# The last quarter of an HBM-to-HBM copy in 8 KB stretches in place of 32 KB

## The chip, the cores and the metric

The kernel runs on one core of a Trainium2 chip. The metric is device time in microseconds, the median of several runs. A profile of one execution, taken by the hardware profiler, stands beside it. It records every instruction and every packet that the core's 16 DMA engines move.

## The reference, and what it computes

A mixture-of-experts layer gives each token a position in its expert's buffer, and drops tokens whose position is not under the capacity. The reference is two lines:

```python
mask = token_positions < capacity          # (16, 1024) int, capacity 256
return (x * mask[..., np.newaxis]).astype(np.float32)   # x: (16, 1024, 512) float32
```

The positions are drawn from 0 to 255, so on these inputs every token is kept, and the output equals x: 33.55 MB to be read and as many to be written.

## The kernel before, in words

The kernel bets on that. It copies x to the output straight from HBM to HBM (HBM is the chip's main memory), without passing through a compute engine. Meanwhile it counts the kept tokens, and only if one is dropped does it go over the data again.

*The copy (L77 to L83).* The 16,384 tokens are laid out as 128 rows of 128 tokens, each token 512 floats, so a row is 256 KB of consecutive bytes. One transfer takes C = 16 tokens of every row: 128 stretches of 32 KB, 256 KB apart, 4 MB together. Eight of them cover the tensor. They go in turn to the two hardware queues that engines own: even ones are issued by SyncE (sp; queue q1 in the profile), odd ones by ScalarE (act; queue q10). All of them raise one semaphore, s_copy, by 16 each when they have landed.

*The order.* The copies and the load of the positions (L72, on ScalarE, ahead of its first copy) are collected in the list "early" and moved to the front of the program (L86 to L95), ahead of the barriers that start the other engines. So each of the two engines issues its transfers one after another and then meets the others at these barriers (L189 and L41 in the profile). Nothing else decides the order. A transfer waits for no other, and the queues may work on them as fast as they can.

*The decision (L97 to L139).* VectorE compares the positions with the capacity (ge, lt, low, keep at L103 to L115), sums keep along each row (kept, L119), TensorE adds up the 128 rows (total, L123), and VectorE makes a flag of it (drop_i, L125). SyncE, ScalarE and VectorE each load the flag (L133) and branch on it. The branch (L140 to L161) would load 4 MB at a time through SBUF (the on-chip memory), multiply by keep and store it, after waiting for the whole copy. Here it is never taken, and no instruction of it stands in the profile.

*The end (L164 to L172).* GpSimd clears the semaphores, waits until s_copy has its full count, 16 times the number of copies, and takes that count off again (L172). That wait is the end of the program.

Of the kernel before, what the change touches and what calls it, by code (L numbers as in the profile page):

```python
# [1 line left out]

# [4 lines left out]


@with_exitstack
def kernel(  # L10
    ctx: ExitStack,
    tc: tile.TileContext,
    x: bass.AP,
    token_positions: bass.AP,
    capacity: bass.AP,
    out: bass.AP,
):
    nc = tc.nc
    P = nc.NUM_PARTITIONS
    fp32 = mybir.dt.float32  # L20
    i32 = mybir.dt.int32
    Alu = mybir.AluOpType

    x_f = x.flatten_outer_dims()
    out_f = out.flatten_outer_dims()
    N, D = x_f.shape
    n_per_p = N // P
    cap = float(int(capacity))
    x_r = x_f.rearrange("(p n) d -> p n d", p=P)
    out_r = out_f.rearrange("(p n) d -> p n d", p=P)  # L30
    tp_i32 = token_positions.rearrange("b s -> (b s)").bitcast(i32)

    sp = nc.sync
    act = nc.scalar
    ve = nc.vector
    pe = nc.tensor
    gp = nc.gpsimd


    tc.close()  # L40
    tc.compile()  # L41

    def sbuf(name, shape, dtype):
        return ctx.enter_context(nc.sbuf_tensor(name, shape, dtype)).ap()

    tp = sbuf("tp", [P, 2 * n_per_p], i32)
    ge = sbuf("ge", [P, n_per_p], fp32)
    lt = sbuf("lt", [P, n_per_p], fp32)
    low = sbuf("low", [P, n_per_p], fp32)
    keep = sbuf("keep", [P, n_per_p], fp32)  # L50
    kept = sbuf("kept", [P, 1], fp32)
    ones = sbuf("ones", [P, 1], fp32)
    drop_i = sbuf("drop_i", [1, 1], i32)
    total = ctx.enter_context(nc.psum_tensor("total", [1, 1], fp32)).ap()
    F = 16
    NBUF = 2
    n_fix = n_per_p // F
    xts = [sbuf(f"xt{b}", [P, F, D], fp32) for b in range(NBUF)]

    s_copy = nc.alloc_semaphore("s_copy")  # L60
    s_tp = nc.alloc_semaphore("s_tp")
    s_ve = nc.alloc_semaphore("s_ve")
    s_pe = nc.alloc_semaphore("s_pe")
    s_ld = [nc.alloc_semaphore(f"s_ld{b}") for b in range(NBUF)]
    s_mul = nc.alloc_semaphore("s_mul")
    s_st = [nc.alloc_semaphore(f"s_st{b}") for b in range(NBUF)]
    s_done = nc.alloc_semaphore("s_done")

    n_copy = 0
    early = []  # L70

    load_tp = act.dma_start(out=tp, in_=tp_i32.rearrange("(p w) -> p w", p=P))  # L72
    early.append(load_tp.then_inc(s_tp, 16).ins)

    C = 16  # L77
    for k in range(n_per_p // C):
        ins = (sp, act)[k % 2].dma_start(
            out=out_r[:, k * C : (k + 1) * C, :], in_=x_r[:, k * C : (k + 1) * C, :]  # L80
        ).then_inc(s_copy, 16)
        early.append(ins.ins)
        n_copy += 1  # L83


    home = nc.cur_bb.bb  # L86
    first_bb = nc.cur_f.blocks[0]
    first_sp = next(
        k for k, i in enumerate(first_bb.instructions) if i.engine == mybir.EngineType.SP
    )  # L90
    names = [i.name for i in early]
    home.instructions = [i for i in home.instructions if i.name not in names]
    first_bb.instructions = (
        first_bb.instructions[:first_sp] + early + first_bb.instructions[first_sp:]
    )  # L95

    lo = tp[:, 0 : 2 * n_per_p : 2]  # L97
    hi = tp[:, 1 : 2 * n_per_p : 2]


    ve.memset(ones, 1.0).then_inc(s_ve, 1)  # L101
    ve.wait_ge(s_tp, 16)
    ve.tensor_scalar(  # L103
        out=ge, in0=lo, scalar1=0.0, scalar2=None, op0=Alu.is_ge
    ).then_inc(s_ve, 1)
    ve.wait_ge(s_ve, 2)
    ve.scalar_tensor_tensor(  # L107
        out=lt, in0=lo, scalar=cap, in1=ge, op0=Alu.is_lt, op1=Alu.mult
    ).then_inc(s_ve, 1)
    ve.wait_ge(s_ve, 3)  # L110
    ve.scalar_tensor_tensor(  # L111
        out=low, in0=hi, scalar=0.0, in1=lt, op0=Alu.is_equal, op1=Alu.mult
    ).then_inc(s_ve, 1)
    ve.wait_ge(s_ve, 4)
    ve.scalar_tensor_tensor(  # L115
        out=keep, in0=hi, scalar=0.0, in1=low, op0=Alu.is_lt, op1=Alu.add
    ).then_inc(s_ve, 1)
    ve.wait_ge(s_ve, 5)
    ve.tensor_reduce(  # L119
        out=kept, in_=keep, axis=mybir.AxisListType.X, op=Alu.add  # L120
    ).then_inc(s_ve, 1)
    pe.wait_ge(s_ve, 6)
    pe.matmul(out=total, lhsT=ones, rhs=kept, start=True, stop=True).then_inc(s_pe, 1)  # L123
    ve.wait_ge(s_pe, 1)
    ve.tensor_scalar(  # L125
        out=drop_i, in0=total, scalar1=float(N) - 0.5, scalar2=None, op0=Alu.is_lt
    ).then_inc(s_ve, 1)


    for e in (sp, act, ve):  # L130
        e.wait_ge(s_ve, 7)
    ET = mybir.EngineType
    drop = nc.values_load(  # L133
        drop_i[0:1, 0:1],
        engines=[ET.SP, ET.Activation, ET.DVE],
        min_val=0,
        max_val=1,
        skip_runtime_bounds_check_because="a comparison gives 0 or 1",
    )  # L139
    with nc.If(drop):  # L140
        for u in range(n_fix):
            b = u % NBUF
            if u >= NBUF:
                sp.wait_ge(s_st[b], 16 * (u // NBUF))
            sp.dma_start(out=xts[b], in_=x_r[:, u * F : (u + 1) * F, :]).then_inc(s_ld[b], 16)
            ve.wait_ge(s_ld[b], 16 * (u // NBUF + 1))
            for j in range(F):
                c = u * F + j
                ve.tensor_scalar(
                    out=xts[b][:, j, :],  # L150
                    in0=xts[b][:, j, :],
                    scalar1=keep[:, c : c + 1],
                    scalar2=None,
                    op0=Alu.mult,
                ).then_inc(s_mul, 1)
            if u == 0:
                act.wait_ge(s_copy, 16 * n_copy)
            act.wait_ge(s_mul, (u + 1) * F)
            act.dma_start(out=out_r[:, u * F : (u + 1) * F, :], in_=xts[b]).then_inc(s_st[b], 16)
        for b in range(NBUF):  # L160
            act.wait_ge(s_st[b], 16 * (n_fix // NBUF))  # L161


    for e in (sp, act, ve):  # L164
        e.sem_inc(s_done, 1)
    gp.wait_ge(s_done, 3)
    own = [s_tp, s_ve, s_pe, *s_ld, s_mul, *s_st, s_done]
    ids = sorted(s.num for s in own)
    assert ids == list(range(ids[0], ids[-1] + 1))
    gp.sem_clear(range(ids[0], ids[-1] + 1))  # L170
    gp.wait_ge(s_copy, 16 * n_copy)
    gp.sem_inc(s_copy, -16 * n_copy)  # L172


# [1 line left out]
_INS = ['x', 'token_positions', 'capacity']  # L176
_OUTS = [((16, 1024, 512), 'float32')]

_NUMBERS = {'capacity': 256}


# [26 lines left out]
```

## Time and profile before

| What | Value |
|---|---|
| Time, median of 3 runs | 104.15 us (103.99 to 104.38) |
| Span of the profiled execution | 104.3 us |
| Busy: VectorE, TensorE, GpSimd | 1.5, 0.2, 0.2 us |
| DMA packets, bytes, mean rate | 1297, 33.69 MB, 323 GB/s |
| Queue q1 (SyncE's), q10 (ScalarE's) | 48.6%, 49.4% of 16 engines' span |
| From issue to landing of a copy, shortest, median, longest | 25.0, 65.2, 101.7 us |

A DMA rate in this profile counts each byte once, though a copy from HBM to HBM reads and writes it. The share of a queue is the time that its packets took, over the span of all 16 DMA engines. The packet records have a start and a duration each. A 4-byte packet is a semaphore's increment, sent by each engine at the end of its part of a transfer. Time from issue to landing is long, because all transfers are issued in the first microseconds and stand in line.

### The profile page before, as it was taken

The page shows a single profiled execution, that of the slowest core. Times are in us where ns is not written, and L with a number is a line of the kernel's source. Part 1 is how long each engine was busy: PE and PEld are TensorE (multiplying, and loading weights), DVE is VectorE, ACT ScalarE, POOL GpSimd, SP SyncE. Part 2 cuts the span into 40 slices and gives each one's busy share as a digit, 9 for nine tenths or more (in the row PEclk, how much of TensorE's full clock was granted, in tenths as well). Part 3 has the DMA queues.
Part 4 walks back from the last instruction along what each step waited for, and adds up shares of the span by engine and source line. Part 5 has one row for each costly group of instructions (what it writes and reads, how often), then busy time and mean ns, then how long its engine had stood idle before and what let it go on. Part 6 is the DMA issues. An engine that isn't in the chain of part 4 may idle for free. (4 is left out here: it accounts for less than half of the span.)

```text
span 104.3 us, 70 instructions
## 1 busy us (share of the span) xinstructions
PE 0.2 (0%) x2; PEld 0.1 (0%) x2; DVE 1.5 (1%) x7; POOL 0.2 (0%) x4
## 2 busy tenths in 40 slices
PE   0000000000000000000000000000000000000000
PEld 0000000000000000000000000000000000000000
DVE  0230000000000000000000000000000000000000
POOL 0000000000000000000000000000000000000000
DMA  8999989989989989999899997998997999989984
GB/s 251 402 352 302 339 280 339 339 302 352 339 289 390 314 276 377 289 327 352 289 364 327 302 377 239 377 377 289 352 327 276 377 327 314 390 276 327 364 277 163
DMA packets 1297, 33.69 MB, mean 323 GB/s; under 512 B 144, under 2 KB 272, under 8 KB 272
## 3 DMA queue, kind: packets, MB, share of 16 engines
q10 hardware_dynamic: 720, 16.91, 49.4%
q1 hardware_dynamic: 576, 16.78, 48.6%
q14 instruction: 1, 0.01, 0.0%
HBM read 33.69 MB, written 33.55 MB: 645 GB/s over the span
## 5 line engine op out<-in xcount | busy, mean ns | idle before, releaser
L107 DVE SCALAR_TENSOR_TENSOR lt<-tp,ge 128x128 f32<-128x128 int32 x1 | 0.3, 293 | 0.0
L111 DVE SCALAR_TENSOR_TENSOR low<-tp,lt 128x128 f32<-128x128 int32 x1 | 0.3, 291 | 0.0
L115 DVE SCALAR_TENSOR_TENSOR keep<-tp,low 128x128 f32<-128x128 int32 x1 | 0.3, 291 | 0.0
L119 DVE TENSOR_REDUCE kept<-keep 128x1 f32<-128x128 f32 x1 | 0.3, 286 | 0.0
L103 DVE TENSOR_SCALAR ge<-tp 128x128 f32<-128x128 int32 x1 | 0.2, 228 | 0.0
L123 PE MATMUL total<-kept,ones 128*1 128x1 f32 x2 | 0.2, 164 | 6.2 <-DVE kept L119 6.2
L125 DVE TENSOR_SCALAR drop_i<-total 1x1 int32<-1x1 f32 x1 | 0.1, 145 | 0.3 <-PE total L123 0.3
L101 DVE MEMSET ones<- 128x1 f32 x1 | 0.1, 59 | 4.6 <-PEq L41 4.6
L189 POOL MEMSET const-bfloat16-1.0<- 128x1 bf16 x1 | 0.1, 101 | 0.0
L189 POOL MEMSET const-uint8-127<- 128x1 uint8 x1 | 0.1, 101 | 0.0
L189 POOL MEMSET const-float32-0.0<- 128x1 f32 x1 | 0.1, 98 | 0.2 <-issue 0.2
L189 POOL MEMSET const-float32-1.0<- 128x1 f32 x1 | 0.1, 98 | 0.0
L123 PEld LDWEIGHTS total<-kept,ones 128*1 128x1 f32 x2 | 0.1, 80 | 6.2 <-DVE kept L119 6.2
## 6 DMA issues: line engine op xcount, KB each, us to landing
out_dram<-in_x_dram SPq DMA_DIRECT2D x4, 4096.0 KB, 62.2
out_dram<-in_x_dram ACTq DMA_DIRECT2D x4, 4096.0 KB, 68.1
tp<-in_token_positions_dram ACTq DMA_DIRECT2D x1, 128.0 KB, 2.1
```

The costliest lines, as they stand in the source:

```text
L101: ve.memset(ones, 1.0).then_inc(s_ve, 1)
L103: ve.tensor_scalar(out=ge, in0=lo, scalar1=0.0, scalar2=None, op0=Alu.is_ge).then_inc(s_ve, 1)
L107: ve.scalar_tensor_tensor(out=lt, in0=lo, scalar=cap, in1=ge, op0=Alu.is_lt, op1=Alu.mult).then_inc(s_ve, 1)
L111: ve.scalar_tensor_tensor(out=low, in0=hi, scalar=0.0, in1=lt, op0=Alu.is_equal, op1=Alu.mult).then_inc(s_ve, 1)
L115: ve.scalar_tensor_tensor(out=keep, in0=hi, scalar=0.0, in1=low, op0=Alu.is_lt, op1=Alu.add).then_inc(s_ve, 1)
L119: ve.tensor_reduce(out=kept, in_=keep, axis=mybir.AxisListType.X, op=Alu.add).then_inc(s_ve, 1)
L123: pe.matmul(out=total, lhsT=ones, rhs=kept, start=True, stop=True).then_inc(s_pe, 1)
L125: ve.tensor_scalar(out=drop_i, in0=total, scalar1=float(N) - 0.5, scalar2=None, op0=Alu.is_lt).then_inc(s_ve, 1)
L189: nc = _bacc.Bacc("TRN2", target_bir_lowering=False, num_devices=1)
```

## The change: the last quarter in short stretches

The first six transfers stay as they are. The last two, one on each queue, become eight of 4 tokens a row, four on each queue: 128 stretches of 8 KB, 1 MB together. The order of the bytes, the queues in turn and the semaphore are as before, and the final wait counts 14 transfers in place of 8. On the other engines, and inside the branch, no instruction changes. The idea is that the copy ends in finer pieces: the last work of each DMA engine is a packet of a quarter of the size.

```diff
-    C = 16
-    for k in range(n_per_p // C):
-        ins = (sp, act)[k % 2].dma_start(
-            out=out_r[:, k * C : (k + 1) * C, :], in_=x_r[:, k * C : (k + 1) * C, :]
-        ).then_inc(s_copy, 16)
-        early.append(ins.ins)
+    at = 0
+    for k, c in enumerate([16] * 6 + [4] * 8):
+        ins = (sp, act)[k % 2].dma_start(out=out_r[:, at : at + c, :], in_=x_r[:, at : at + c, :])
+        early.append(ins.then_inc(s_copy, 16).ins)
+        at += c
         n_copy += 1
+    assert at == n_per_p
```

## The prediction

> **What bounds the kernel now.** I read the page first: busy time by engine, then the row of DMA shares and rates, then the queues and the list of issues.
>
> ```profile
> PE 0.2 (0%) x2; PEld 0.1 (0%) x2; DVE 1.5 (1%) x7; POOL 0.2 (0%) x4
> ...
> DMA  8999989989989989999899997998997999989984
> ...
> q10 hardware_dynamic: 720, 16.91, 49.4%
> q1 hardware_dynamic: 576, 16.78, 48.6%
> ...
> HBM read 33.69 MB, written 33.55 MB: 645 GB/s over the span
> ...
> out_dram<-in_x_dram SPq DMA_DIRECT2D x4, 4096.0 KB, 62.2
> out_dram<-in_x_dram ACTq DMA_DIRECT2D x4, 4096.0 KB, 68.1
> ```
>
> The compute engines work for 2 of 104.3 us. The 16 DMA engines are at 8 or 9 tenths in every slice but the last. The two queues split the copy evenly, and their packets fill 98% of sixteen engines' span. So this is a copy at a rate, and the question is what the change does to that rate in the last quarter and to the last slice (the 4). Then the timeline, to see what stands ahead of the copy and what the other engines do:
>
> ```profile
> 0.00 2.94 SPq L79 DMA_DIRECT2D out_dram<-in_x_dram  x4
> 0.13 0.39 ACTq L72 DMA_DIRECT2D tp<-in_token_positions_dram  x1
> ...
> 0.56 2.70 ACTq L79 DMA_DIRECT2D out_dram<-in_x_dram  x4
> ...
> 6.46 0.14 DVE L125 TENSOR_SCALAR drop_i<-total 1x1 int32<-1x1 f32 x1 [0.28 <-PE total L123]
> ```
>
> All eight copies are issued by 3.3 us, and the whole decision on drops is over by 6.6 us. The chain of waits ends there too: after drop_i nothing but the final wait on s_copy is left, which the page can't draw as a chain, since what it waits for is DMA. The only later instruction is GpSimd's subtraction at L172, at 104.28 us. Last, the stretches by quarter:
>
> ```profile
> 0.00:26.00 26.00, 0.19 (x2) 0.09 (x2) 1.54 (x7) 0.20 (x4) 1.00 0.98 327
> 26.00:52.00 26.00, 0.00 (x0) 0.00 (x0) 0.00 (x0) 0.00 (x0) 1.00 0.99 324
> 52.00:78.00 26.00, 0.00 (x0) 0.00 (x0) 0.00 (x0) 0.00 (x0) 1.00 1.01 333
> 78.00:104.00 26.00, 0.00 (x0) 0.00 (x0) 0.00 (x0) 0.00 (x0) 1.00 0.95 313
> ```
>
> The last two columns are the DMA share and GB/s (by the time at which a packet starts). The rate is level, with no slow stage. The last quarter is a little under, because no packet starts in its last microsecond.
>
> The trace's packet records say more. Each of the 1024 stretches of 32 KB is one packet, 64 to an engine, and one engine's packet starts as its last one ends. The fastest took 1.21 us (27 GB/s), the mean is 1.59 us. So an engine spends about 0.38 us of each packet held up by something that it shares. Sorted by start, the packets come in groups of 16 from one queue, then 16 from the other: the engines take turns between q1 and q10, one packet each, and all keep within 1.0 to 1.5 us of each other. The last sixteen packets end between 103.19 and 103.90 us, mean 103.50; the last semaphore lands at 104.26, 0.36 us after the last byte's packet.
>
> **What the Trainium skill says.** "DMA: Bandwidth & Descriptors", section Issuing engines are not separate DMA queues: transfers from both issuing engines run on the same 16 DMA engines and interleave, so a second queue saves only issue time. The trace agrees: groups of 16 in turn, and about 334 GB/s between 100 and 102 us, when q10 is alone, against 323 over the span. The same page, section Why small descriptors are slow, has a fixed cost for each packet inside the engine, which counts most when packets are short. Section Latency and other measured facts has a row on the pitch of rows: copies of 16 KiB rows lose rate at large power-of-two pitches (207 GB/s at 512 KiB and 164 at 2 MiB, against 214 with a padded pitch). Here rows are 256 KiB apart, and if an engine takes eight neighbouring rows, engines are 2 MiB apart; no run here shows what pitch does. "HBM Reference", section Specifications (TRN2), gives about 716 GB/s for the memory that a pair of cores share. The trace's 645 GB/s of reads and writes is 90% of it, so the shared thing that holds the engines up is probably the memory.
>
> **The change part by part.**
>
> *Issue.* Each queue has three 4 MB copies and four of 1 MB in place of four of 4 MB: three more issues each. One takes 0.58 to 0.99 us in the trace (median 0.62 on SyncE, 0.65 on ScalarE), so both are done by about 5.3 us in place of 3.3. Behind them on these two engines stands the barrier ahead of the decision (VectorE starts at 4.64 us), so the decision moves from 6.6 to about 8.6 us. Nobody waits for it: the copy is in flight, and GpSimd's final wait ends at 104 us. If instead the queues took only some of these transfers at a time, an issue would wait until an earlier transfer lands; the third pair lands at about 76 and 82 us, and 20 us would be left for the decision. Cost nothing, hidden behind the copy.
>
> *Semaphore packets.* Six more transfers add 6 of the 4-byte packets to each engine, 9 ns each in the records: 0.05 us. In the trace no data packet waits at such a border: one starts as the 4-byte packet ends.
>
> *The fixed cost of a packet.* The last quarter is 16 packets of 32 KB for each engine; it becomes 64 of 8 KB: 48 more. The trace of before has no 8 KB packet of the copy, so I bound it. The fastest 32 KB packet, 1211 ns for 32,768 B, is at most 37 ps a byte. Upper end: instruction fetches are 8 KB packets and took 324 ns at best. Straight through (8192 B, 324) and (32768 B, 1211) the slope is 36.1 ps per byte and the fixed part 324 − 296 = 28 ns. 48 × 28 = 1.34 us. Lower end: the position load's packets of 1 KB took 44 ns at best; 44 − 37 = 7 ns, 48 × 7 = 0.34 us. I take the middle, 17.5 ns: 0.84 us. It would be on the path, since each engine always has its next packet. What could hide it is the 0.38 us in each 32 KB that the engines wait for the memory: an engine that loses 17 ns leaves its share to others. I don't count on this whole, because 1.21 us packets occur all through the span (9% are under 1.23 us), so at any time some engines run at their own limit.
>
> *The end.* Sixteen engines finish their fixed shares over 0.71 us, 0.40 us from mean to last. That is the most that evening out can give. Shorter packets don't move work between engines, so I take a third, −0.14 us. The 0.36 us from last packet to landing stays.
>
> *Memory locality.* A stretch of 8 KB visits four times as many rows for the same bytes. Unknown; zero in the forecast, ends in the rivals.
>
> Sum: 0 + 0.05 + 0.84 − 0.14 = +0.75 us on 104.15: 104.9 us.
>
> **The rivals.**
>
> *Hidden: no change.* The memory sets the rate and swallows the fixed cost. For: 645 of 716 GB/s, mean packet 1.59 against 1.21 us. Against: nothing direct; it is nearly as likely as the forecast. 104.15 + 0.05 − 0.14 = 104.1 us.
>
> *Faster, the other side.* Short stretches keep the engines closer together, and closeness goes with speed. For: the second and third groups, when the engines start within 0.43 us of each other, took 1.23 and 1.39 us on average, while later groups, 1.0 to 1.5 us apart, took 1.60. If the last 16 groups' worth ran like the third, 16 × (1.60 − 1.39) = 3.4 us would go; a fifth of it, 0.7 us, with the end's 0.14, gives 103.3 us. Against: these groups are also the first ones, when the memory has little on hand yet, and only one queue runs.
>
> *Much slower: rows that collide.* With 8 KB stretches all engines read and write in the same 8 KB of every 256 KB for a whole transfer, and spread themselves over a quarter of the addresses that they have now. Between the pitch row's losses, 3% and 23%, I take 8% of the last quarter: 26 × 0.08 = 2.1 us, 106.3 us. Against: the first groups, in closest step at the same offsets, were the fastest, so being in step over neighbouring addresses doesn't hurt in itself.
>
> **How the numbers follow.** Forecast 0.30, hidden 0.27, faster 0.29, collision 0.14. Slower by over 0.5% (above 104.67) is the forecast and the collision, 0.44; within 0.5% is hidden, 0.27; faster (below 103.63) 0.29. The time is the forecast's, 104.9. The range takes in hidden, the fixed cost's upper end (104.15 + 0.05 + 1.34 = 105.5), most of the faster case (to 103.2) and the mild half of the collision (to 106.3); outside it lie a faster case that gains over a fifth, and a collision over 8%, together under 0.2.
>
> **What the changed profile would show.** The queues' packets: 768 of 32 KB and 1024 of 8 KB, 96 more of 4 B; the issues over by about 5.3 us and drop_i by about 8.6. The rate up to 76 us should be as before (324 to 333 GB/s by quarter). In the last quarter the forecast wants some 317 to 325 GB/s and an 8 KB packet of 0.41 to 0.42 us on average (a quarter of 1.59 is 0.40), the hidden case 0.40, the faster case 0.39 or less, the collision 0.43 or more. The last packets should end within less than 0.71 us of each other. The prediction fails if the memory likes or dislikes short stretches by more than a packet costs, or if a queue runs dry between the short transfers, which would show as gaps in the DMA row after 76 us.

## The result and the profile after

The changed kernel takes 104.64 us (104.40 to 104.73, 6 runs) against 104.28 us (103.99 to 104.38, 6 runs) for the kernel before: ratio 1.0037, 95% interval 1.0020 to 1.0053, so 0.2 to 0.55 us slower. Timed once more later, with more runs, the ratio was 1.0021 (1.0007 to 1.0034).

The lines of the page after that answer to those shown of before:

```profile
PE 0.2 (0%) x2; PEld 0.1 (0%) x2; DVE 1.5 (1%) x7; POOL 0.2 (0%) x4
...
DMA  7998989989969989989799799899899999999995
...
q10 hardware_dynamic: 1152, 16.91, 48.9%
q1 hardware_dynamic: 1008, 16.78, 48.8%
...
HBM read 33.69 MB, written 33.55 MB: 654 GB/s over the span
...
out_dram<-in_x_dram SPq DMA_DIRECT2D x3, 4096.0 KB, 48.7
out_dram<-in_x_dram ACTq DMA_DIRECT2D x3, 4096.0 KB, 54.6
out_dram<-in_x_dram SPq DMA_DIRECT2D x4, 1024.0 KB, 89.6
out_dram<-in_x_dram ACTq DMA_DIRECT2D x4, 1024.0 KB, 90.8
```

Each queue has 432 packets more: 384 data packets and 48 of 4 bytes. The DMA row stays at 8 or 9 tenths through the last quarter, up to its last slice, so the engines don't run dry between the short transfers. The timeline after:

```profile
0.00 4.73 SPq L79 DMA_DIRECT2D out_dram<-in_x_dram  x7
...
0.56 4.55 ACTq L79 DMA_DIRECT2D out_dram<-in_x_dram  x7
...
8.31 0.15 DVE L125 TENSOR_SCALAR drop_i<-total 1x1 int32<-1x1 f32 x1 [0.28 <-PE total L123]
```

The issues now end at 5.1 us in place of 3.3, and the decision follows 1.85 us later. Nobody waits for it.

One thing needs care. The span here is 102.8 us, less than the 104.3 of the profile before, though the kernel is slower. In the runs of both kernels the time is the span plus 1.9 us, so the times of before mean spans of 102.1 to 102.5: its profile caught an execution 1.9 us longer than its timed ones. I therefore took a second profile of the kernel before (the first experiment below) and compare rates by stretch. First the kernel after, then that second profile of before, each from 10 to 40, 40 to 75, 80 to 90 and 90 to 100 us; the last columns are DMA share and GB/s:

```profile
10.00:40.00 30.00, 0.00 (x0) 0.00 (x0) 0.00 (x0) 0.00 (x0) 1.00 1.00 333
40.00:75.00 35.00, 0.00 (x0) 0.00 (x0) 0.00 (x0) 0.00 (x0) 1.00 0.99 331
80.00:90.00 10.00, 0.00 (x0) 0.00 (x0) 0.00 (x0) 0.00 (x0) 1.00 1.01 331
90.00:100.00 10.00, 0.00 (x0) 0.00 (x0) 0.00 (x0) 0.00 (x0) 1.00 0.99 330
```

```profile
10.00:40.00 30.00, 0.00 (x0) 0.00 (x0) 0.00 (x0) 0.00 (x0) 1.00 1.01 332
40.00:75.00 35.00, 0.00 (x0) 0.00 (x0) 0.00 (x0) 0.00 (x0) 1.00 0.99 330
80.00:90.00 10.00, 0.00 (x0) 0.00 (x0) 0.00 (x0) 0.00 (x0) 1.00 1.04 347
90.00:100.00 10.00, 0.00 (x0) 0.00 (x0) 0.00 (x0) 0.00 (x0) 1.00 0.96 321
```

The short stretches run at 330 to 331 GB/s, as fast as the long ones ahead of them. (The 347 and 321 of the second fence average 334; a packet counts whole in the stretch where it starts.) The packet records agree: in the kernel after, a 32 KB packet took 1560 ns on average and an 8 KB packet 390.7, which is a quarter of 1563. From the moment that three quarters of the bytes have moved to the end of the span it takes 26.08 us after, and 26.21 and 26.23 in the two profiles of before. So whatever the change costs is too small to be seen in one profile. It had to be made larger.

### The profile page after: what moved, and what is told of

Its sections match the earlier page's. It is cut to its first block, busy times and chain, and to the rows that moved or that the text cites. A ratio compares the mean times of both kernels' runs of the same rounds, so it can differ in the third digit from the quotient of the medians.

```text
span 102.8 us, 76 instructions
## 1 busy us (share of the span) xinstructions
PE 0.2 (0%) x2; PEld 0.1 (0%) x2; DVE 1.5 (1%) x7; POOL 0.2 (0%) x4
## 3 DMA queue, kind: packets, MB, share of 16 engines
q10 hardware_dynamic: 1152, 16.91, 48.9%
q1 hardware_dynamic: 1008, 16.78, 48.8%
```

## The experiments

Theories when they began: *packets* (each has a fixed cost), *transfers* (each more costs something at its border), *locality* (going to another row with every 8 KB), and *hidden* (the memory sets the rate and swallows the packet's cost). From the records of the kernel after, the fixed cost first looked like 8.3 ns: the fast 8 KB packets took 309 ns, the fastest of 32 KB 1211, hence 36.7 ps a byte and 8.3 ns over. (That was read too high: 23 of the copy's 1024 packets of 8 KB took 307 ns, with which the same sum gives 5.7.)

**The kernel before again**, unchanged.

> The kernel before, unchanged, for a second profile. The changed kernel's time is its span plus 1.88 us in every run, and the profile of before has a span of 104.3 us where its times, 103.99 to 104.38, less 1.9 us, want 102.1 to 102.5. If that profile caught a long execution, this one has a span of about 102.4 us, a mean 32 KB packet of about 1.555 us in place of 1.589, and a ratio of 1.000.

Ratio 0.9991 (0.9974 to 1.0008). The span was 103.4 us, 1 us over what I expected, because on this chip both copies take 105.1 to 105.2 us; time and span are 1.9 us apart here too, so the first profile had caught a long execution (106.2 us). The mean 32 KB packet took 1571 ns. The levels of chips differ by nearly 1 us, so only ratios within one comparison count below. I call this the first chip; the next three experiments ran on it as well.

**Short stretches, no more transfers.**

```diff
-for k in range(8): ... x_r[:, k * 16 : (k + 1) * 16, :]
+for k in range(6): ... x_r[:, k * 16 : (k + 1) * 16, :]
+for h in range(2): ... x_r[:, 96:128, :] as "p (b h c) d -> p b h (c d)", b=4, h=2, part [:, :, h, :]
```

> Eight transfers as before, but the last two, of 4 MB each, take every second 8 KB stretch of the last 64 KB of each row: 8 KB packets with no added transfer or semaphore packet, and with each engine staying in one row for four packets. Packet theory (a fixed 8.3 ns for each packet, from the fastest 8 KB packet of 309 ns and the fastest 32 KB packet of 1211 ns; 48 more for each engine): +0.40 us, ratio 1.004. Transfer theory (0.36 us for six more transfers and what they do at borders): ratio 1.000. Locality theory (rows visited four times as often): near 1.000, since four packets in turn stay in one row.

Ratio 0.9997 (0.9983 to 1.0012). A packet cost of 8.3 ns on the path falls: 48 of them would be +0.40 us, and the interval ends at +0.13.

**More transfers, no short stretches.**

```diff
+for g in range(4):
+    for n in (96, 112): ... x_r[g * 32 : (g + 1) * 32, n : n + 16, :]
```

> The last quarter in eight transfers of 1 MB as in the change, but each of 32 rows by 32 KB, so that all packets stay at 32 KB: 14 transfers, no more data packets. Packet theory: ratio 1.000. Transfer theory: +0.36 us, ratio 1.0035. Locality theory: 1.000.

Ratio 0.9995 (0.9982 to 1.0009). Six more transfers cost at most 0.1 us.

**Everything in 8 KB stretches.**

```diff
-for k, c in enumerate([16] * 6 + [4] * 8):
+for k, c in enumerate([4] * 32):
```

> The whole copy in 32 transfers of 8 KB stretches, 16 on each queue: 192 more packets for each engine and 24 more transfers than before. Packet theory: 192 x 8.3 ns = +1.6 us, ratio 1.015. Transfer theory: 24 x 0.06 = +1.4 us. Locality theory: four times the change's 0.36, +1.4 us. If the cost is one of the end alone (the last packets, or the step from long to short stretches), +0.4 us or less.

Ratio 1.0014 (0.9997 to 1.0031), +0.15 us. All the theories with a linear cost had asked for 1.4 us or more. Each of them falls at the size that I had given it; on this chip a mostly hidden cost is left.

**The changed kernel again.**

> The changed kernel, unchanged, timed again in more runs. The first comparison gave 1.0037 from six runs of each. With all of the copy in 8 KB stretches the ratio was 1.0014 (0.9997 to 1.0031), with more of every suspected cost. If the change has a cost of its own (the step from long to short stretches on two queues out of step, or the end), the ratio is 1.0035 to 1.004 again. If the first value was mostly chance or one chip's, it is 1.000 to 1.0015.

Ratio 1.0021 (1.0007 to 1.0034), 22 runs against 36, on a second chip, as the next three experiments. The change comes out slower once more, by less than at first, though the two intervals overlap: neither expectation holds quite.

**The last quarter in 2 KB stretches**, `[16] * 6 + [1] * 32`.

> The last quarter in 32 transfers of 2 KB stretches: 240 more packets for each engine than before and 26 more transfers. Packet theory, unhidden: 240 x 8.3 ns = +2.0 us, ratio 1.019. Hidden theory (the memory sets the rate as long as sixteen 2 KB packets at their fastest, 16 x (75 + 8) = 1.34 us, stay under the 1.57 us that 32 KB takes on average): ratio 1.000 to 1.003. If each transfer costs 0.06 us at its border: +1.6 us, 1.015.

Ratio 1.0085 (1.0055 to 1.0115), +0.9 us: over what fully hidden allows, under half of the 2.0 us that 8.3 ns would cost.

**Half of the DMA engines: a first attempt**, in 32 KB and in 8 KB stretches.

```diff
+o8, x8 = out_f, x_f as "(a b n) d -> a b (n d)", a=8, b=16
+... out=o8[:, :, w], in_=x8[:, :, w]
```

> The whole copy in eight transfers of 32 KB stretches whose outer dimension is 8, so that only 8 of the 16 DMA engines carry it, 128 packets each. This takes the load off the memory. Hidden theory: packets run at the engine's own limit, mean 1.21 to 1.25 us, time about 2 + 128 x 1.22 = 158 us, ratio 1.50. If instead each engine is held up by its own queue and not by the others, the mean stays at 1.57 us and the time is about 203 us, ratio 1.93.

> The same on 8 engines in 32 transfers of 8 KB stretches: 384 more packets for each engine. Hidden theory: with no wait for the memory to hide in, the fixed cost shows, 384 x 8.3 ns = +3.2 us over the 8-engine kernel of 32 KB stretches, packets of about 0.31 us. If packets carry no fixed cost, or if it is hidden here too, the two are equal within 0.5 us.

The premise failed: 8 groups of 16 rows with one pitch are 128 rows of one pitch, and all 16 engines worked (queue shares of 48.9% and 49.1%), so these were once more the packets of the kernel before (0.9979, 0.9960 to 0.9999) and of the kernel all in 8 KB (1.0070, 1.0045 to 1.0095, 5 runs). The first is a warning: with the same packets as before its interval leaves out 1, and it lies as far below it as the changed kernel lay above it on this chip. A ratio within 0.2% of 1 thus says little alone. The second is of use all the same: the same transfers gave 1.0014 on one chip and 1.0070 on another, with intervals that don't meet. The cost of short stretches thus depends on the chip or the occasion.

**Half of the DMA engines.** On the first chip again, as the experiment after these two. Taking 8 of the 16 rows of a group at a time keeps the dimensions apart.

```diff
+b = slice(k // 2 % 2 * 8, k // 2 % 2 * 8 + 8)
+... out=o8[:, b, w], in_=x8[:, b, w]
```

> The whole copy on 8 of the 16 DMA engines: 16 transfers of 8 groups of 8 rows, one group to an engine, in 32 KB stretches, 128 packets for each engine. (The two kernels before that were meant to do this ran on 16, since their rows merged into one dimension of 128.) The load on the memory falls by half. Hidden theory: packets run at the engine's own limit, mean 1.21 to 1.25 us, time about 2 + 128 x 1.22 + 2 = 160 us, ratio 1.53. If each engine is held up by itself and not by the others, packets stay at 1.57 us: about 205 us, ratio 1.95.

> The same on 8 engines with 8 KB stretches, 64 transfers, 512 packets for each engine. Hidden theory: without a wait for the memory to hide in, the fixed 8.3 ns of each of 384 more packets shows: +3.2 us over the 8-engine kernel with 32 KB stretches, mean packet 0.309 to 0.315 us. If the fixed cost isn't real, both take the same time within 0.5 us.

162.03 us and 162.97 us (ranges 161.82 to 162.14 and 162.71 to 163.43); ratios to before 1.540 (1.534 to 1.547) and 1.550 (1.543 to 1.557). Span, queues (packets, MB, share of 16 engines' span) and memory traffic, first of 32 KB, then of 8 KB:

```profile
span 159.9 us, 78 instructions
...
q10 hardware_dynamic: 720, 16.91, 24.6%
q1 hardware_dynamic: 576, 16.78, 24.6%
...
HBM read 33.69 MB, written 33.55 MB: 420 GB/s over the span
```

```profile
span 160.9 us, 126 instructions
...
q10 hardware_dynamic: 2448, 16.91, 25.0%
q1 hardware_dynamic: 2304, 16.78, 24.9%
...
HBM read 33.69 MB, written 33.55 MB: 418 GB/s over the span
```

Shares of 49% and 50% say that 8 of 16 engines worked without a break. A 32 KB packet is now 1223 ns on average (0.492 × 16 × 159.9 us over 1024 packets gives 1.23 us) in place of 1571. That settles what kind of thing holds the engines up in the kernel before: something shared, which slows each of sixteen engines and not each of eight. With it gone, 384 more packets for each engine cost 0.94 us: 2.4 ns each (by the scatter of four runs of each I estimate 1.6 to 3.6). The traces put it at the upper end. The middle of both copies, first of 32 KB, then of 8 KB, DMA share and GB/s last:

```profile
10.00:150.00 140.00, 0.10 (x2) 0.00 (x0) 0.15 (x1) 0.00 (x0) 1.00 0.50 216
10.00:150.00 140.00, 0.19 (x2) 0.09 (x2) 1.54 (x7) 0.00 (x0) 1.00 0.51 214
```

By the packet records the bytes from the first tenth to the last tenth took 124.4 and 125.7 us: 1.26 us over 307 added packets, 4.1 ns each. The time of the whole kernel shows less because the first 2% of the bytes took 0.5 us less in the kernel of 8 KB. Durations of records say more still (310.6 ns, four of them 19.6 ns over one of 1223, so 6.5 ns for each added packet). Records overlap a little: nine are open at once on the eight engines for 14 us of the 8 KB kernel, 3 us of the other. A packet's duration isn't what it adds.

**2 KB stretches, no more transfers.**

```diff
+for h in range(2): ... x_r[:, 96:128, :] as "p (b h) d -> p b h d", h=2, part [:, :, h, :]
```

> Eight transfers as before, the last two taking every second 2 KB of the last 64 KB of each row: 240 more packets for each engine, no more transfers, and an engine stays in one row for 16 packets. The kernel with 2 KB stretches in 32 transfers was 1.0085. If that was paid by packets: 1.006 to 1.011 here. If by 26 more transfers or by going to another row with each packet: 1.000 to 1.003.

Ratio 1.0030 (1.0015 to 1.0045), +0.31 us or 1.3 ns for each of 240 packets.

**512 B stretches, no more transfers.** The same with each token cut into four pieces, every second one to a queue.

> Eight transfers, the last two taking every second 512 B of the last 64 KB of each row: 1008 more packets for each engine than before, no more transfers, an engine stays in one row for 64 packets. Small-cost theory (a packet costs 2.4 ns net at the engine's own limit, from 0.94 us over 384 packets on 8 engines; sixteen engines then need 64 x (18.9 + 2.4) = 1.36 us for 32 KB, under the 1.57 us that the memory allows; what shows is the 1.3 ns a packet of the 2 KB kernel): +1.3 us, ratio 1.012, up to 1.023 if the 2.4 ns show whole. Record theory (8.3 ns a packet, as the fastest packets' records say): 64 x 27.2 = 1.74 us for 32 KB, above the memory's 1.57, so at least +2.7 us, ratio 1.026 to 1.08.

Ratio 1.0131 (1.0111 to 1.0150), +1.37 us or 1.36 ns for each of 1008 packets, on a third chip. The small cost is the same with four times the packets, though on another chip, and 8.3 ns is refuted once more. Here it is large enough for the profile to show, in the page's packet line and the same four stretches as above:

```profile
DMA packets 17425, 33.69 MB, mean 323 GB/s; under 512 B 144, under 2 KB 16656, under 8 KB 16656
```

```profile
10.00:40.00 30.00, 0.00 (x0) 0.00 (x0) 0.00 (x0) 0.00 (x0) 1.00 0.99 330
40.00:75.00 35.00, 0.00 (x0) 0.00 (x0) 0.00 (x0) 0.00 (x0) 1.00 1.00 334
80.00:90.00 10.00, 0.00 (x0) 0.00 (x0) 0.00 (x0) 0.00 (x0) 1.00 1.05 314
90.00:100.00 10.00, 0.00 (x0) 0.00 (x0) 0.00 (x0) 0.00 (x0) 1.00 1.07 320
```

From 80 to 100 us the rate is 4 to 5% lower; if that holds for the 25 us of the short stretches, it is 1.0 to 1.3 us. The DMA share is over 1 in both stretches because records overlap: more than sixteen are open at once for 20 us of this kernel, 4 us of the second profile of before.

All runs with added packets side by side, us over before divided by the packets added to each engine:

| Kernel | Added packets, transfers | Added us (95%) | ns a packet |
|---|---|---|---|
| 8 engines, 8 KB against 32 KB, first chip | 384, 48 | 0.94 (about 0.6 to 1.4) | 2.4 |
| 512 B, in the row, third chip | 1008, 0 | 1.37 (1.16 to 1.57) | 1.4 |
| 2 KB, in the row, first chip | 240, 0 | 0.31 (0.16 to 0.47) | 1.3 |
| 8 KB, in the row, first chip | 48, 0 | −0.03 (−0.18 to 0.13) | within ±4 |
| all 8 KB, first chip | 192, 24 | 0.15 (−0.03 to 0.33) | 0.8 |
| all 8 KB, second chip | 192, 24 | 0.73 (0.47 to 1.00) | 3.8 |
| last quarter 2 KB, second chip | 240, 26 | 0.89 (0.58 to 1.21) | 3.7 |
| the change, again, second chip | 48, 6 | 0.22 (0.07 to 0.36) | 4.6 |
| the change, first comparison, chip not on record | 48, 6 | 0.39 (0.21 to 0.55) | 8.0 |

## Why the prediction was right, and where it was off

*What bounds the kernel.* Right. The copy is held up by something that the engines share: with 8 engines a 32 KB packet falls from 1.57 to 1.22 us. (The DMA row was read a little too well: two slices ahead of the last are at 7 tenths.) That it is the memory is an argument still (654 GB/s in the kernel after, of the 716 that the Trainium skill's "HBM Reference", section Specifications (TRN2), gives); no run tells the memory from the path to it.

*Issue.* Right: 5.1 us for 5.3, drop_i done at 8.46 for 8.6, nothing on the path.

*Semaphore packets.* 96 more of 4 bytes, as said. Six transfers by themselves changed nothing (0.9995, 0.9982 to 1.0009).

*The fixed cost of a packet.* The mechanism stands; this term was mis-sized. The step "I take the middle, 17.5 ns: 0.84 us. It would be on the path" had two faults. The size came from few single records: the best of seven instruction fetches, 324 ns, gave the upper end, where fetches in other profiles and the copy's own 8 KB packets took 307 ns at best, and even these records overlap. Measured at the engines' own limit, with 8 engines, the cost is 2.4 ns by the time of the whole kernel and 4.1 ns by its steady middle. And on the first chip it is probably hidden in part: with all 16 engines 1.3 ns show in the kernel of 2 KB stretches in the row (0.7 to 2.0, so by whole times alone the intervals touch), and 1.4 ns on the third chip in that of 512 B. The sentence that it hides in the 0.38 us for which an engine waits in each 32 KB, which I wrote and then discounted, deserved more weight there. On the second chip nothing is seen to hide: 3.7 to 4.6 ns a packet. For the change I estimate from these 48 × 1.3 = 0.06 to 48 × 4.1 = 0.20 us, not 0.84.

*The end.* "I take a third, −0.14 us" isn't seen. From the mean to the last of the sixteen engines' ends it is 0.48 us in the kernel after and 0.40 in its second profile; in the first profile of before 0.40, in its second 0.69. From first to last they lie 0.82 us apart (101.60 to 102.42), so the sign that I had named, under 0.71, didn't come. The differences are no larger than the scatter from one execution to the next. By their last semaphore packets both queues now end 0.62 us apart, where q1 was 2.9 us ahead of q10, and that brought nothing: one queue alone had kept all the engines busy.

*The sum.* +0.75 us was forecast, +0.36 measured, with an interval that excludes both zero and the forecast. Slower was the right side, and the range held the time. But the range was 3 us wide, for an effect of 0.4, and 0.37% lies in the band within 0.5%, to which I had given 0.27 under the name of hidden; the likeliest band, slower by over 0.5%, was missed. The signs point the same way: in the last quarter some 331 GB/s and 0.391 us for an 8 KB packet, where the forecast wanted 317 to 325 and 0.41 to 0.42. So the side was right and the size was not, and a range that took in most of the rivals too would have held nearly any outcome; that it held says little for the mechanism.

*The rivals.* Hidden (104.1 us) is the nearest in mechanism, a little too low in time. Faster falls, since with short stretches the rate stays at 331 GB/s. Its reason, closeness, isn't tested by this: sixteen packets in turn do start within some 0.3 to 0.5 us of each other, in place of 0.8 to 1.4, but with packets of 0.39 us they could hardly do otherwise. The collision falls too, at the size of 8%: all in 8 KB stretches costs 0.1 to 0.7%.

*What stays open.* The change came out 0.22 and 0.39 us slower, and added packets explain 0.06 to 0.20. The kernels that also go to another row with every short packet, in more and smaller transfers, paid 3.7 to 4.6 ns a packet on the second chip, and 0.8 on the first. So rows, transfers together with short packets, and the chip are tangled: no two of these kernels that differ in rows alone ran on one chip, and a kernel that changes rows without more transfers wasn't run. That the same transfers gave 1.0014 and 1.0070 shows that a part belongs to the chip or the occasion, and the chip alone could account for all of it: on the first no 16-engine kernel paid over 1.3 ns a packet, on the second none under 3.7, but the kernels that stay in the row weren't run on the second; how large a part of the change's 0.2 to 0.4% that is, the runs don't tell.

## What to carry to other kernels

Where sixteen DMA engines shared a limit, finer pieces neither sped up nor evened out the end of the copy: every engine had work until about the last microsecond, and 0.4 us was all that there was to gain. They cost little as well, from about 1 to about 4 ns for each added packet, depending on the chip or the occasion. At 8 KB that is under 1% even for the whole copy; 512 B in a quarter of it cost 1.3%. To price a packet, add many of them and divide the difference in time, on more than one chip; durations of single records gave 8.3 and 17.5 ns.

## What the runs showed of the hardware that was not expected

*A queue takes only so much ahead.* With 19 copies on each queue (last quarter in 2 KB stretches) the early issues take 0.6 us each, but SyncE's tenth starts at 6.1 us and ends at 39.3 (in the profiled execution, the longest of the six at 107.0 us). The issues end only at 88 us, and the decision waits behind them:

```profile
0.00 88.08 SPq L79 DMA_DIRECT2D out_dram<-in_x_dram  x19
...
0.55 87.78 ACTq L79 DMA_DIRECT2D out_dram<-in_x_dram  x19
...
91.57 0.14 DVE L125 TENSOR_SCALAR drop_i<-total 1x1 int32<-1x1 f32 x1 [0.28 <-PE total L123]
```

That is 12 us short of becoming the end of the kernel. The seven of the change fit. The 512 B kernel's issues were all over by 3.2 us, though its last two copies have 8192 stretches each, so it isn't simply the number of pieces. With the whole copy in 8 KB, 16 copies on each queue, ten issues of SyncE are over by 7.0 us and the others take over 5 us each. What frees the room isn't shown: in the 2 KB kernel the first copy of SyncE's queue had ended at 23.7 us, and the tenth issue waited on.

*Eight engines copy at two thirds of the rate of sixteen:* 162.0 us against 105.1, 214 GB/s against 331.
